# Spreading the score levels of a pair of heads over the next pair's projections in a one-core HGRN2 block

## The chip, the cores and the metric

The kernel runs on one core of one Trainium2 chip, in fp32. The metric is device time in microseconds (us) of one execution. TensorE (PE) does the matmuls, VectorE (DVE), ScalarE (ACT) and GpSimd (POOL) the elementwise work, and SyncE (SP) issues the DMAs of the part looked at here. Each engine runs its own list of instructions strictly in order and waits on semaphores for what the others have to deliver.

## The reference

One block of a diffusion transformer, batch 1, 512 tokens, width 2048. Cut to what matters here:

```
px = modulate(x, sh1, sc1) @ w_in          # q, v, f forward, f backward, g, pool, conv
k   = (1 - lb) * sigmoid(-z);  f = lb + (1 - lb) * sigmoid(z)     # forget gates, both directions
# HGRN2, 8 heads of 128, both directions, on silu(q):
S_t = f_t * S_(t-1) + k_t v_t^T ;  o_t = q_t S_t ;  o = o_f + flip(o_b)
o   = rmsnorm(o) * norm_w * silu(g)
loc = [pool_mixer(px_pool), px_bg * dwconv3(px_cg * px_h)]      # rows of 64 tokens
yx  = [o, loc] @ w_out                     # 1024 + 512 + 512 columns
x   = layer_norm(ALPHA * x + g1 * yx);  conv FFN;  layer_norm
mod = silu(c) @ w_ada + b_ada              # sh1, sc1, g1, sh2, sc2, g2
```

## The kernel before

The program is one long run of stages, and the change lies in one of them, from about 380 to 1054 us of the span: the heads and the local mixers. In it PE computes the projections of `x`, 256 columns at a time. One projection (`proj_x`) has four quarters; a quarter loads 512 rows of weights (`wload`: a DMA to `wr`, a rounded copy `wh` on ACT, the rest `wl` on DVE), calls `background()`, and then issues its matmuls. Each product of fp32 numbers is three matmuls (`mm3`, lines 111 to 113), so a quarter has 24 matmuls of 512 columns, or 48 of 256 columns for `v`, whose result has the tokens on the partitions.

The heads are taken in four pairs. A pair has the projections q, v, g, f forward and f backward (the first pair's v and f were computed in an earlier stage, so it has q and g alone). After them comes the attention of the pair (`gla`, a generator for each head). It builds the 128x128 score blocks from seven **levels** m = 1, 2, 4, ... 64. At a level:

- ACT copies the keys of the level into `kc` (L569), PE makes the scores `lv` from `kc` and `Q` (L573, four matmuls of 128x128), and DVE writes them under a mask into `A` (`copy_predicated`, L648; at m = 1 ACT writes `A` and DVE adds the diagonal `dg`);
- DVE multiplies `Q` by the decays `T` (L589), POOL does the same to the two halves of `K` (L592, L593), and DVE multiplies pairs of decays into the next, half as long `T` (L594). The next level of the head needs `Q` and `K` of this one.

Behind the levels there is a **tail** of five steps: the keys are transposed (`kTp`, L605), the state increments `U` and the states `S` made (L611, L617), the output `o` (L625 to 627), its norm `on` on ACT and DVE (L636), the transpose `oT` (L641) and `ot` (L643).

In `heads` both heads' seven levels are issued in one go, when the pair's projections have been issued. The tails are run by `background()`, one step at each quarter of the next projections, the second head three quarters behind the first (TAIL_LAG). The scheduler may move instructions within what the data allow, and puts some matmuls of the next projection between the levels.

`background()` also draws three steps at each quarter from `ada_rest`, which computes the later columns of `mod`: a step is a 256 KB load `a` on SP's queue into one of six buffers and one DVE instruction `aacc` (L688, the first of a group of sixteen L686); each group ends in small matmuls `a2r`, `a2c`.

Behind the last pair come `local` (two pool projections with their window sums, then two groups of conv projections cg, ch, cb) and `split_o`, which splits the 16 tiles of the output for the last projection.

Of the kernel before, what the change touches and what calls it, by code (L numbers as in the profile page):

```python
# [36 lines left out]
TAIL_LAG = 3  # L37
# [35 lines left out]
class Kernel:  # L73
# [436 lines left out]
    def heads(self, xp, gp, T0, V0):  # L510
        nc = self.nc
        for p in range(4):
            qs, Qs, gs = [], [], []
            b = self.proj_x(f"q{p}", 256 * p)
            for h in range(2):
                sg = gp.tile([P, L], F32, name=f"sq_{p}_{h}", tag="sig", bufs=1)
                nc.scalar.activation(out=sg, in_=b[h], func=AF.Sigmoid)
                q = gp.tile([P, L], F32, name=f"q_{p}_{h}", tag="q", bufs=2)
                nc.vector.tensor_tensor(out=q, in0=b[h], in1=sg, op=ALU.mult)
                qs.append(q)  # L520
            if p == 0:
# [12 lines left out]
            if p > 0:
                T = [xp.tile([P, 2, L], F32, name=f"T_{2 * p + h}", tag="t", bufs=2) for h in range(2)]
            K = [xp.tile([P, 2, L], F32, name=f"K_{2 * p + h}", tag="k", bufs=2) for h in range(2)]
            for d in range(2):
                zs = [t[:, 1 - d] for t in T]
                if p > 0:
                    zs = self.proj_x(f"f{d}{p}", DH * (2 + d) + 256 * p)  # L540
                for h in range(2):
                    self.gates(zs[h], T[h], K[h], d, d * H + 2 * p + h)
            for h in range(2):
                Q = gp.tile([P, 2, L], F32, name=f"Q_{p}_{h}", tag="Q", bufs=2)
                nc.vector.tensor_tensor(out=Q, in0=vw(qs[h][:, :], [[0, 2], [1, L]]), in1=T[h], op=ALU.mult)
# [12 lines left out]
    def gla(self, gp, hd, q, Q, K, T, V, gs):
# [179 lines left out]

    def local(self, gp):
        nc, I = self.nc, self.I  # L740
        pw = gp.tile([P, 4, P], F32, name="pool_w", tag="q", bufs=2)
        nc.sync.dma_start(out=pw, in_=I["pool_w"][0].rearrange("g p q -> p g q"))
        inv = gp.tile([P, 4, 64], F32, name="inv", tag="inv", bufs=1)
        nc.sync.dma_start(out=inv, in_=I["k_inv"])
        R = L // 64
        for p in range(2):
            b = self.proj_x(f"pool{p}", 5 * DH + 256 * p)
            for i in range(2):
                g = 2 * p + i
                win = POOL_WINDOWS[g]  # L750
                W = 64 + win
                pad = gp.tile([P, R, W], F32, name=f"pad_{g}", tag="Q", bufs=2)
                nc.gpsimd.memset(pad, 0.0)
                nc.vector.tensor_copy(out=pad[:, :, win // 2:win // 2 + 64],
                                      in_=b[i].rearrange("p (r t) -> p r t", t=64))
                src, s = pad, 1

                tmp = gp.tile([P, R, W], F32, name=f"win_{g}", tag="Q", bufs=2)
                sums = tmp
                wlen = W  # L760
                while s < win:
                    wlen -= s
                    nc.vector.tensor_tensor(out=sums[:, :, 0:wlen], in0=src[:, :, 0:wlen], in1=src[:, :, s:s + wlen],
                                            op=ALU.add)
                    src = sums
                    s *= 2
                dd = gp.tile([P, R, 64], F32, name=f"pd_{g}", tag="gs", bufs=2)
                nc.vector.tensor_tensor(out=dd, in0=sums[:, :, 0:64], in1=vw(inv[:, g], [[0, R], [1, 64]]), op=ALU.mult)
                nc.vector.tensor_tensor(out=dd, in0=dd, in1=pad[:, :, win // 2:win // 2 + 64], op=ALU.subtract)
                py = self.glbank(f"py_{g}")  # L770
                nc.tensor.matmul(out=py, lhsT=pw[:, g], rhs=dd.rearrange("p r t -> p (r t)"), start=True, stop=True)
                o = gp.tile([P, L], F32, name=f"op_{g}", tag="o", bufs=16)
                nc.scalar.activation(out=o, in_=py, func=AF.Copy, scale=self.cols["pool_scale"][:, g:g + 1])
                self.o[H + g] = o
        cw = self.cols["conv_w"]
        base = 5 * DH + 512
        for p in range(2):
            b = self.proj_x(f"cg{p}", base + 512 + 256 * p)
            cg = []
            for i in range(2):  # L780
                t = gp.tile([P, L], F32, name=f"cg_{p}_{i}", tag="A", bufs=2)
                nc.scalar.copy(out=t, in_=b[i])
                cg.append(t)
            b = self.proj_x(f"ch{p}", base + 1024 + 256 * p)
            ys = []
            for i in range(2):
                n = 2 * p + i
                nc.vector.tensor_tensor(out=cg[i], in0=b[i], in1=cg[i], op=ALU.mult)
                y = gp.tile([P, L], F32, name=f"cy_{p}_{i}", tag="o", bufs=16)
                nc.scalar.activation(out=y, in_=cg[i], func=AF.Copy, scale=cw[:, 4 + n:5 + n])  # L790
                c3 = cg[i].rearrange("p (r t) -> p r t", t=64)
                y3 = y.rearrange("p (r t) -> p r t", t=64)
                nc.vector.scalar_tensor_tensor(out=y3[:, :, 1:64], in0=c3[:, :, 0:63], scalar=cw[:, n:n + 1],
                                               in1=y3[:, :, 1:64], op0=ALU.mult, op1=ALU.add)
                nc.vector.scalar_tensor_tensor(out=y3[:, :, 0:63], in0=c3[:, :, 1:64], scalar=cw[:, 8 + n:9 + n],
                                               in1=y3[:, :, 0:63], op0=ALU.mult, op1=ALU.add)
                ys.append(y)
            b = self.proj_x(f"cb{p}", base + 256 * p)
            for i in range(2):
                nc.vector.tensor_tensor(out=ys[i], in0=b[i], in1=ys[i], op=ALU.mult)  # L800
                self.o[H + 4 + 2 * p + i] = ys[i]
# [373 lines left out]
    def run(self):  # L1175
# [76 lines left out]
```

## Time and profile before

| what | value |
| --- | --- |
| median of three executions | 2699.03 us (2696.9 to 2702.64) |
| profiled execution: its time, its span | 2703.39 us, 2701.6 us |
| PE busy in the span | 2573.6 us (95%) |
| DVE / ACT / POOL busy | 1895.1 (70%) / 941.6 (35%) / 225.7 us (8%) |
| PE's granted clock, mean | 0.989 |
| chain that ended last, largest shares | PE 69%, DVE 14%, DMA 8%, issue 5% |

Times in rows are counted from the span's start. A row of the timeline gives start and length of an instruction (or of a run of like ones), its engine and source line, and in brackets how long the engine stood idle ahead of it and what ended that. The end of a matmul is modelled: one follows another closer than its length. The granted clock is given as a share of full speed.

### The profile page before, as it was taken

The page shows a single profiled execution, that of the slowest core. Times are in us where ns is not written, and L with a number is a line of the kernel's source. Part 1 is how long each engine was busy: PE and PEld are TensorE (multiplying, and loading weights), DVE is VectorE, ACT ScalarE, POOL GpSimd, SP SyncE. Part 2 cuts the span into 40 slices and gives each one's busy share as a digit, 9 for nine tenths or more (in the row PEclk, how much of TensorE's full clock was granted, in tenths as well). Part 3 has the DMA queues.
Part 4 walks back from the last instruction along what each step waited for, and adds up shares of the span by engine and source line. Part 5 has one row for each costly group of instructions (what it writes and reads, how often), then busy time and mean ns, then how long its engine had stood idle before and what let it go on. Part 6 is the DMA issues. An engine that isn't in the chain of part 4 may idle for free.

```text
span 2701.6 us, 40017 instructions
## 1 busy us (share of the span) xinstructions
PE 2573.6 (95%) x16332; PEld 2261.4 (84%) x16332; DVE 1895.1 (70%) x2390; ACT 941.6 (35%) x1127; POOL 225.7 (8%) x207
## 2 busy tenths in 40 slices
PE   5999999999999999989979999999999999999996
PEld 4677978878787787868879999999999988888885
DVE  5534689696968735688888888888888864434338
ACT  4222443232323224444644443443443433222111
POOL 0111022040404000000100000000000000000004
PEclk9999999999999999999989999999999999999998
DMA  8755356646463534666633333333333374333321
GB/s 265 250 194 187 121 198 199 218 136 214 138 221 131 169 97 160 204 213 212 189 104 125 126 103 124 122 106 119 109 122 114 117 245 161 136 121 119 118 94 63
DMA packets 311125, 416.15 MB, mean 154 GB/s; under 512 B 17860, under 2 KB 200476, under 8 KB 310428
## 3 DMA queue, kind: packets, MB, share of 16 engines
q1 hardware_dynamic: 310940, 413.59, 46.6%
q8 instruction: 128, 2.10, 0.3%
q14 instruction: 57, 0.47, 0.0%
HBM read 393.59 MB, written 19.93 MB: 153 GB/s over the span
## 4 chain that ended last, share of the span: by engine, by line
PE 69%; DVE 14%; DMA 8%; issue 5%; ACT 2%; POOL 1%; SPq 1%; DVEq 0%; ACTq 0%; POOLq 0%
PE dn L113 5%; PE dn L112 5%; PE dn L111 5%; PE ub_g L111 3%; PE ub_g L113 3%; PE ub_g L112 3%; DMA W_u<-in_w_up_dram 3%; PE ub_u L111 3%; PE ub_u L113 3%; PE ub_u L112 3%; DMA W_g<-in_w_up_dram 2%; DVE L_g L973 2%; PE wo L112 2%; PE wo L111 2%; PE wo L113 2%
## 5 line engine op out<-in xcount | busy, mean ns | idle before, releaser
L973 DVE TENSOR_TENSOR L_dn<-W_dn,H_dn 128x1536 fp32r<-128x1536 f32 (+1 forms) x56 | 96.2, 1718 | 207.9 <-ACT H_dn L972 207.9
L972 ACT CAST H_u<-W_u 128x1792 fp32r<-128x1792 f32 x80 | 134.1, 1692 | 230.2 <-DVE W_u L991 158.2
L688 DVE SCALAR_TENSOR_TENSOR aacc<-a,csil,aacc 128x512 f32<-128x512 f32 x240 | 180.2, 751 | 12.9 <-DMA a<-in_w_ada_dram 7.5
L973 DVE TENSOR_TENSOR L_u<-W_u,H_u 128x1792 fp32r<-128x1792 f32 x80 | 161.6, 2020 | 38.0 <-ACT H_u L972 38.0
L111 PE MATMUL dn<-H_dn,hh 128*128 128x512 f32 x480 | 186.4, 389 | 1.4 <-ACT hh L1070 1.4
L112 PE MATMUL dn<-L_dn,hh 128*128 128x512 f32 x480 | 187.0, 390 | 0.0
L113 PE MATMUL dn<-H_dn,hl 128*128 128x512 f32 x480 | 186.7, 390 | 0.0
L972 ACT CAST H_g<-W_g 128x1792 fp32r<-128x1792 f32 x80 | 135.2, 1695 | 123.4 <-DVE W_g L991 46.0
L972 ACT CAST H_dn<-W_dn 128x1536 fp32r<-128x1536 f32 (+1 forms) x56 | 81.3, 1451 | 276.2 <-PE dn L113 275.3
L973 DVE TENSOR_TENSOR L_g<-W_g,H_g 128x1792 fp32r<-128x1792 f32 x80 | 161.4, 2018 | 2.4 <-ACT H_g L972 2.4
L111 PE MATMUL ub_g<-h2h,H_g 128*128 128x256 f32 x480 | 135.6, 283 | 14.9 <-ACT H_g L972 14.9
L125 POOL TENSOR_TENSOR ln_r<-ln_e,mhalf 128x1 f32<-128x1 f32 x12 | 9.3, 784 | 1636.0 <-DVE ln_e L120 1405.6
L113 PE MATMUL ub_g<-h2h,L_g 128*128 128x256 f32 x480 | 135.5, 283 | 4.5 <-DVE L_g L973 4.5
L113 PE MATMUL ub_u<-h2h,L_u 128*128 128x256 f32 x480 | 134.3, 280 | 4.4 <-DVE L_u L973 4.4
L112 PE MATMUL ub_g<-h2l,H_g 128*128 128x256 f32 x480 | 134.9, 281 | 0.0
L111 PE MATMUL ub_u<-h2h,H_u 128*128 128x256 f32 x480 | 134.6, 280 | 0.0
L112 PE MATMUL ub_u<-h2l,H_u 128*128 128x256 f32 x480 | 133.9, 279 | 0.0
L106 DVE TENSOR_TENSOR wl_wo<-wr_wo,wh_wo 128x1024 fp32r<-128x1024 f32 x64 | 78.3, 1223 | 49.4 <-ACT wh_wo L105 49.3
L111 PEld LDWEIGHTS dn<-H_dn,hh 128*128 128x128 f32 x480 | 90.1, 188 | 20.6 <-ACT hh L1070 1.8
L113 PEld LDWEIGHTS dn<-H_dn,hl 128*128 128x128 f32 x480 | 90.1, 188 | 19.3 <-DVE hl L1071 0.6
L112 PE MATMUL wo<-wl_wo,oh 128*128 128x512 f32 x256 | 102.7, 401 | 3.7 <-DVE wl_wo L106 3.6
L112 PEld LDWEIGHTS dn<-L_dn,hh 128*128 128x128 f32 x480 | 90.1, 188 | 19.2 <-DVE L_dn L973 0.4
(445 smaller groups left out, 8370.7 us busy)
## 6 DMA issues: line engine op xcount, KB each, us to landing
a<-in_w_ada_dram SPq DMA_DIRECT2D x256, 256.0 KB, 4.3
W_g<-in_w_up_dram SPq DMA_DIRECT2D x80, 512.0 KB, 4.6
W_u<-in_w_up_dram SPq DMA_DIRECT2D x80, 512.0 KB, 4.6
W_dn<-in_w_down_dram SPq DMA_DIRECT2D x24, 1536.0 KB, 6.8
wr_wo<-in_w_out_dram SPq DMA_DIRECT2D x64, 512.0 KB, 4.4
ada<-in_w_ada_dram SPq DMA_DIRECT2D x56, 512.0 KB, 5.0
wr_r<-in_w_in_dram SPq DMA_DIRECT2D x48, 512.0 KB, 3.7
wr_up<-in_w_up_dram SPq DMA_DIRECT2D x32, 512.0 KB, 4.5
```

Source lines behind the costliest of these rows:

```text
L106: (lo_engine or nc.vector).tensor_tensor(out=lo, in0=raw, in1=hi.bitcast(F32), op=ALU.subtract)
L111: mm(out=out, lhsT=st[0], rhs=mv[0], start=start, stop=False)
L112: mm(out=out, lhsT=st[0], rhs=mv[1], start=False, stop=False)
L113: mm(out=out, lhsT=st[1], rhs=mv[0], start=False, stop=stop)
L125: nc.gpsimd.tensor_tensor(out=r, in0=t, in1=self.mhalf[:, 0:n], op=ALU.pow)
L688: nc.vector.scalar_tensor_tensor(out=acc, in0=raw, scalar=self.csil[:, k:k + 1], in1=acc, op0=ALU.mult, op1=ALU.add)
L972: nc.scalar.copy(out=H[:, 0:n], in_=src)
L973: nc.vector.tensor_tensor(out=Lw[:, 0:n], in0=src, in1=H[:, 0:n].bitcast(F32), op=ALU.subtract)
```

## The change

The two generators of a pair are no longer driven through their levels in `heads`. They are kept in `self.steps`, and `background()` advances them: in each of the next seven quarters both heads make one level, after that the tails follow as before, one step a quarter, the second head three quarters behind. So the levels of pair 0, 1 and 2 lie beside q and v of the following pair, and those of the last pair beside the first conv projections. `local` is cut in two functions and its order becomes conv 0, pool 0, pool 1, conv 1.

The rest makes room for what now lives longer: `q` and `g` tiles come from the 16 buffers of the outputs (tag "o"), `pool_w` and `pd` have buffers of their own, and the conv's `cg` lies in tiles of a pool that the split of the outputs uses too. What is computed is the same.

```diff
@@ heads
-                q = gp.tile([P, L], F32, name=f"q_{p}_{h}", tag="q", bufs=2)
+                q = gp.tile([P, L], F32, name=f"q_{p}_{h}", tag="o", bufs=16)
...
-                g = gp.tile([P, L], F32, name=f"g_{p}_{h}", tag="gs", bufs=2)
+                g = gp.tile([P, L], F32, name=f"g_{p}_{h}", tag="o", bufs=16)
...
-            steps = [self.gla(gp, 2 * p + h, qs[h], Qs[h], K[h], T[h], V[:, :, h * P:(h + 1) * P], gs[h])
-                     for h in range(2)]
-            for _ in range(len(LEVELS)):
-                for st in steps:
-                    next(st)
-            self.tails, self.bg_calls = steps, 0
-        for st in self.tails:
-            for _ in st:
-                pass
+            self.steps = [self.gla(gp, 2 * p + h, qs[h], Qs[h], K[h], T[h], V[:, :, h * P:(h + 1) * P], gs[h])
+                          for h in range(2)]
+            self.bg_calls = 0
@@ background
-        if self.tails:
-            next(self.tails[0], None)
-            if self.bg_calls >= TAIL_LAG:
-                next(self.tails[1], None)
-            self.bg_calls += 1
+        n, self.bg_calls = self.bg_calls, self.bg_calls + 1
+        if self.steps:
+            next(self.steps[0], None)
+            if n < len(LEVELS) or n >= len(LEVELS) + TAIL_LAG:
+                next(self.steps[1], None)
         self.bg_due += 3.0
@@ local
-        pw = gp.tile([P, 4, P], F32, name="pool_w", tag="q", bufs=2)
+        pw = gp.tile([P, 4, P], F32, name="pool_w", tag="pw", bufs=1)
...
+        self.conv(gp, 0)
+        self.pool(gp, 0, pw, inv)
+        self.pool(gp, 1, pw, inv)
+        self.conv(gp, 1)
...
-                dd = gp.tile([P, R, 64], F32, name=f"pd_{g}", tag="gs", bufs=2)
+            dd = gp.tile([P, R, 64], F32, name=f"pd_{g}", tag="pd", bufs=2)
...
-                t = gp.tile([P, L], F32, name=f"cg_{p}_{i}", tag="A", bufs=2)
+            t = self.a2(f"cg_{p}_{i}", F32)
@@ run
                     self.local(gp)
-                    for _ in self.bg:
-                        pass
+                    for st in (self.bg, *self.steps):
+                        for _ in st:
+                            pass
                     self.split_o()
```

What this does to PE's list behind pair 0 is shown by the rows around level 2 of heads 0 and 1 (`lv_0_2`, `lv_1_2`); `px_q1_0` and `px_q1_1` are the two banks of the next pair's q projection, and a name ends in a running number. Before:

```order
L573 MATMUL lv_0_2_3698<-Q_0_0_3648,kc_0_2_3696 128x128 x4
L573 MATMUL lv_1_2_3710<-Q_0_1_3650,kc_1_2_3708 128x128 x4
L113 MATMUL px_q1_1_3841<-hxh_0_354,wl_x_q1_0_3845 128x512
L111 MATMUL px_q1_0_3840<-hxh_1_639,wh_x_q1_0_3844 128x512
L112 MATMUL px_q1_0_3840<-hxl_1_640,wh_x_q1_0_3844 128x512
L113 MATMUL px_q1_0_3840<-hxh_1_639,wl_x_q1_0_3845 128x512
L573 MATMUL lv_0_4_3722<-Q_0_0_3648,kc_0_4_3720 128x128 x4
L111 MATMUL px_q1_1_3841<-hxh_1_639,wh_x_q1_0_3844 128x512
L573 MATMUL lv_1_4_3734<-Q_0_1_3650,kc_1_4_3732 128x128 x4
```

and after the change:

```order
L111 MATMUL px_q1_1_3653<-hxh_3_756,wh_x_q1_0_3656 128x512
L112 MATMUL px_q1_1_3653<-hxl_3_757,wh_x_q1_0_3656 128x512
L113 MATMUL px_q1_1_3653<-hxh_3_756,wl_x_q1_0_3657 128x512
L567 MATMUL lv_0_2_3748<-Q_0_0_3648,kc_0_2_3746 128x128 x4
L567 MATMUL lv_1_2_3760<-Q_0_1_3650,kc_1_2_3758 128x128 x4
L111 MATMUL px_q1_0_3652<-hxh_4_1003,wh_x_q1_1_3742 128x512
L112 MATMUL px_q1_0_3652<-hxl_4_1004,wh_x_q1_1_3742 128x512
```

Level 2 now stands behind the whole first quarter (24 matmuls, three of them shown; before it stood behind three), and 24 matmuls of the next quarter lie between it and level 4, where four lay.

On DVE the same place reads, before:

```order
L648 COPY_PREDICATED A_0_3652<-masks_652,lv_0_2_3698 128x512
L589 TENSOR_TENSOR Q_0_0_3648<-Q_0_0_3648,T2_0_3653 128x128x2x2
L648 COPY_PREDICATED A_1_3674<-masks_652,lv_1_2_3710 128x512
L589 TENSOR_TENSOR Q_0_1_3650<-Q_0_1_3650,T2_1_3675 128x128x2x2
L594 TENSOR_TENSOR T_1_270<-T2_1_3675 128x2x128
L648 COPY_PREDICATED A_0_3652<-masks_652,lv_0_4_3722 128x512
L589 TENSOR_TENSOR Q_0_0_3648<-Q_0_0_3648,T_0_269 128x64x2x4
```

and after the change (a2_2_3 is load `a` number 3 of group 2, `wl_x_q1_3` the weights of a later quarter):

```order
L106 TENSOR_TENSOR wl_x_q1_2_3806<-wr_x_q1_2_3803,wh_x_q1_2_3805 128x1024
L642 COPY_PREDICATED A_0_3660<-masks_652,lv_0_2_3748 128x512
L583 TENSOR_TENSOR Q_0_0_3648<-Q_0_0_3648,T2_0_3661 128x128x2x2
L642 COPY_PREDICATED A_1_3682<-masks_652,lv_1_2_3760 128x512
L583 TENSOR_TENSOR Q_0_1_3650<-Q_0_1_3650,T2_1_3683 128x128x2x2
L588 TENSOR_TENSOR T2_0_3661<-T_0_269 128x2x64
L588 TENSOR_TENSOR T2_1_3683<-T_1_270 128x2x64
L683 SCALAR_TENSOR_TENSOR aacc_1_3504<-a2_1_15_3836,csil_154,aacc_1_3504 128x512
L683 SCALAR_TENSOR_TENSOR aacc_2_3839<-a2_2_2_3900,csil_154,aacc_2_3839 128x512
L683 SCALAR_TENSOR_TENSOR aacc_2_3839<-a2_2_3_3903,csil_154,aacc_2_3839 128x512
L683 SCALAR_TENSOR_TENSOR aacc_2_3839<-a2_2_4_3971,csil_154,aacc_2_3839 128x512
L106 TENSOR_TENSOR wl_x_q1_3_3870<-wr_x_q1_3_3867,wh_x_q1_3_3869 128x1024
```

Where the copies and products of one level followed those of the level before at once, there now stand a weight split `wl` and four `aacc` between two levels.

## Rows read from the trace of the kernel before

**Rows 1.** Busy time by stretch. The columns are the stretch, its length, busy us and instructions of PE, of PE's weight load, of DVE, ACT and POOL, PE's granted clock, the share of the DMA engines' time and GB/s. The stretches are the levels of pair 0, the projections of pair 1, and the levels of pairs 1 and 3.

```profile
380.00:430.00 50.00, 44.71 (x259) 37.29 (x258) 46.82 (x72) 15.58 (x25) 25.61 (x27) 0.97 0.45 149
430.00:540.00 110.00, 110.00 (x634) 95.32 (x633) 77.16 (x115) 31.30 (x56) 3.04 (x3) 1.00 0.74 243
540.00:580.00 40.00, 33.88 (x212) 26.97 (x211) 39.88 (x59) 14.76 (x24) 31.74 (x30) 1.00 0.15 45
...
838.00:880.00 42.00, 35.92 (x227) 29.15 (x225) 38.60 (x56) 13.83 (x22) 31.04 (x30) 1.00 0.15 47
```

**Rows 2.** What PE waited for from 380 to 1060 us: idle us in all, number of waits, the longest.

```profile
PE lv L573 <- DVE Q L589: 12.9, 25, 3.6
PE lv L573 <- DVE Q L545: 4.6, 6, 1.1
PE lv L573 <- ACT kc L569: 4.5, 8, 1.6
PE lv L573 <- DVE T L594: 1.9, 3, 0.6
PE oT L641 <- DVE on L636: 1.8, 2, 0.9
```

**Rows 3.** PE's timeline in the levels of pair 1, about level 16.

```profile
563.13 0.40 PE L113 MATMUL px_q<-hxh,wl_x_q 128*128 128x512 f32 x1
563.69 1.13 PE L573 MATMUL lv<-Q,kc 128*128 128x128 f32 x8 [0.16 <-DVE Q L589]
564.57 0.47 PE L111 MATMUL px_q<-hxh,wh_x_q 128*128 128x512 f32 x1
```

**Rows 4.** PE's timeline and the stretches (columns as in rows 1) in pair 0, at level 2.

```profile
399.90 3.52 PE L573 MATMUL lv<-Q,kc 128*128 128x128 f32 x16 [3.59 <-DVE Q L589]
403.08 0.77 PE L113 MATMUL px_q<-hxh,wl_x_q 128*128 128x512 f32 x1
...
404.05 0.39 PE L112 MATMUL px_q<-hxl,wh_x_q 128*128 128x512 f32 x1
...
396.00:400.00 4.00, 0.41 (x3) 0.13 (x2) 4.00 (x5) 0.86 (x2) 4.00 (x4) 1.00 0.41 122
400.00:404.00 4.00, 4.00 (x18) 3.63 (x19) 4.00 (x6) 1.08 (x2) 3.47 (x4) 0.58 0.31 112
```

**Rows 5.** PE's timeline where the levels of pair 1 begin, and one row of pair 3.

```profile
543.76 1.56 PE L573 MATMUL lv<-Q,kc 128*128 128x128 f32 x8 [1.10 <-DVE Q L545]
...
547.12 1.56 PE L573 MATMUL lv<-Q,kc 128*128 128x128 f32 x8 [0.45 <-DVE Q L545]
...
552.16 1.08 PE L573 MATMUL lv<-Q,kc 128*128 128x128 f32 x7 [0.97 <-DVE Q L589]
...
849.96 1.23 PE L573 MATMUL lv<-Q,kc 128*128 128x128 f32 x8 [1.55 <-ACT kc L569]
```

**Rows 6.** DVE's timeline in one level of pair 1, both heads.

```profile
562.12 0.73 DVE L648 COPY_PREDICATED A<-masks,lv 128x512 f32<-128x512 uint8 x1
562.75 0.79 DVE L589 TENSOR_TENSOR Q<-Q,T 128x512 f32<-128x512 f32 x1
563.47 0.66 DVE L594 TENSOR_TENSOR T<-T 128x64 f32<-128x64 f32 x1
564.05 0.73 DVE L648 COPY_PREDICATED A<-masks,lv 128x512 f32<-128x512 uint8 x1
...
565.94 0.73 DVE L648 COPY_PREDICATED A<-masks,lv 128x512 f32<-128x512 uint8 x1
```

**Rows 7.** DVE's and POOL's timelines at the last levels of pair 1.

```profile
576.84 0.67 DVE L589 TENSOR_TENSOR Q<-Q,T 128x512 f32<-128x512 f32 x1
577.43 0.16 DVE L594 TENSOR_TENSOR T<-T 128x8 f32<-128x8 f32 x1
...
569.86 0.62 POOL L592 TENSOR_TENSOR K<-K,T 128x256 f32<-128x256 f32 x1 [0.19 <-DVE T L594]
570.44 1.07 POOL L593 TENSOR_TENSOR K<-K,T 128x256 f32<-128x256 f32 x1
```

**Rows 8.** PE's timeline in a quarter of an f projection and at the end of one of v.

```profile
500.17 0.39 PE L111 MATMUL px_f<-hxh,wh_x_f 128*128 128x512 f32 x1
...
505.61 0.39 PE L111 MATMUL px_f<-hxh,wh_x_f 128*128 128x512 f32 x1
...
597.15 0.28 PE L112 MATMUL px_v<-wl_x_v,hxh 128*128 128x256 f32 x1
597.27 0.28 PE L113 MATMUL px_v<-wh_x_v,hxl 128*128 128x256 f32 x1
```

**Rows 9.** A weight split on DVE's timeline in an f projection, and L688 by its source line (least, median and greatest length in ns).

```profile
505.31 1.23 DVE L106 TENSOR_TENSOR wl_x_f<-wr_x_f,wh_x_f 128x1024 fp32r<-128x1024 f32 x1 [4.22 <-ACT wh_x_f L105]
...
L688 DVE SCALAR_TENSOR_TENSOR aacc<-a,csil,aacc x228: 736/752/1046, 380.1 to 947.8; 128x512 f32<-128x512 f32 x114
```

**Rows 10.** DVE's timeline at the beginning of pair 0's levels.

```profile
394.62 1.05 DVE L688 SCALAR_TENSOR_TENSOR aacc<-a,csil,aacc 128x512 f32<-128x512 f32 x1 [1.70 <-DMA a<-in_w_ada_dram]
395.59 1.88 DVE L106 TENSOR_TENSOR wl_x_q<-wr_x_q,wh_x_q 128x1024 fp32r<-128x1024 f32 x1
397.39 0.68 DVE L532 TENSOR_TENSOR g<-px_g,g 128x512 f32<-128x512 f32 x1
...
398.60 2.63 DVE L589 TENSOR_TENSOR Q<-Q,T 128x512 f32<-128x512 f32 x2
```

More of the change, by code (lines that the diff above doesn't have):

```diff
@@ L744, in local @@
         nc.sync.dma_start(out=inv, in_=I["k_inv"])
-        R = L // 64
[L746 to L766, printed above, removed]
-                dd = gp.tile([P, R, 64], F32, name=f"pd_{g}", tag="gs", bufs=2)
[L768 to L774, printed above, removed]
@@ new lines, in local, with pool @@
+        self.conv(gp, 0)
+        self.pool(gp, 0, pw, inv)
+        self.pool(gp, 1, pw, inv)
+        self.conv(gp, 1)
+    def pool(self, gp, p, pw, inv):
+        nc = self.nc
+        R = L // 64
+        b = self.proj_x(f"pool{p}", 5 * DH + 256 * p)
+        for i in range(2):
+            g = 2 * p + i
+            win = POOL_WINDOWS[g]
+            W = 64 + win
+            pad = gp.tile([P, R, W], F32, name=f"pad_{g}", tag="Q", bufs=2)
+            nc.gpsimd.memset(pad, 0.0)
+            nc.vector.tensor_copy(out=pad[:, :, win // 2:win // 2 + 64],
+                                  in_=b[i].rearrange("p (r t) -> p r t", t=64))
+            src, s = pad, 1
+            tmp = gp.tile([P, R, W], F32, name=f"win_{g}", tag="Q", bufs=2)
+            sums = tmp
+            wlen = W
+            while s < win:
+                wlen -= s
+                nc.vector.tensor_tensor(out=sums[:, :, 0:wlen], in0=src[:, :, 0:wlen], in1=src[:, :, s:s + wlen],
+                                        op=ALU.add)
+                src = sums
+                s *= 2
+            dd = gp.tile([P, R, 64], F32, name=f"pd_{g}", tag="pd", bufs=2)
+            nc.vector.tensor_tensor(out=dd, in0=sums[:, :, 0:64], in1=vw(inv[:, g], [[0, R], [1, 64]]), op=ALU.mult)
+            nc.vector.tensor_tensor(out=dd, in0=dd, in1=pad[:, :, win // 2:win // 2 + 64], op=ALU.subtract)
+            py = self.glbank(f"py_{g}")
+            nc.tensor.matmul(out=py, lhsT=pw[:, g], rhs=dd.rearrange("p r t -> p (r t)"), start=True, stop=True)
+            o = gp.tile([P, L], F32, name=f"op_{g}", tag="o", bufs=16)
+            nc.scalar.activation(out=o, in_=py, func=AF.Copy, scale=self.cols["pool_scale"][:, g:g + 1])
+            self.o[H + g] = o
@@ L775, in local, with conv @@
+    def conv(self, gp, p):
+        nc = self.nc
         cw = self.cols["conv_w"]
         base = 5 * DH + 512
[L777 to L780, printed above, removed]
-                t = gp.tile([P, L], F32, name=f"cg_{p}_{i}", tag="A", bufs=2)
[L782 to L801, printed above, removed]
@@ new lines, in conv @@
+        b = self.proj_x(f"cg{p}", base + 512 + 256 * p)
+        cg = []
+        for i in range(2):
+            t = self.a2(f"cg_{p}_{i}", F32)
+            nc.scalar.copy(out=t, in_=b[i])
+            cg.append(t)
+        b = self.proj_x(f"ch{p}", base + 1024 + 256 * p)
+        ys = []
+        for i in range(2):
+            n = 2 * p + i
+            nc.vector.tensor_tensor(out=cg[i], in0=b[i], in1=cg[i], op=ALU.mult)
+            y = gp.tile([P, L], F32, name=f"cy_{p}_{i}", tag="o", bufs=16)
+            nc.scalar.activation(out=y, in_=cg[i], func=AF.Copy, scale=cw[:, 4 + n:5 + n])
+            c3 = cg[i].rearrange("p (r t) -> p r t", t=64)
+            y3 = y.rearrange("p (r t) -> p r t", t=64)
+            nc.vector.scalar_tensor_tensor(out=y3[:, :, 1:64], in0=c3[:, :, 0:63], scalar=cw[:, n:n + 1],
+                                           in1=y3[:, :, 1:64], op0=ALU.mult, op1=ALU.add)
+            nc.vector.scalar_tensor_tensor(out=y3[:, :, 0:63], in0=c3[:, :, 1:64], scalar=cw[:, 8 + n:9 + n],
+                                           in1=y3[:, :, 0:63], op0=ALU.mult, op1=ALU.add)
+            ys.append(y)
@@ L803, in split_o @@
+        b = self.proj_x(f"cb{p}", base + 256 * p)
+        for i in range(2):
+            nc.vector.tensor_tensor(out=ys[i], in0=b[i], in1=ys[i], op=ALU.mult)
+            self.o[H + 4 + 2 * p + i] = ys[i]
     def split_o(self):
@@ L1193, in run @@
                 with tc.tile_pool(name="gp", bufs=1) as gp:
-                    self.bg, self.bg_due, self.tails = self.ada_rest(gp), 0.0, []
+                    self.bg, self.bg_due, self.steps, self.bg_calls = self.ada_rest(gp), 0.0, [], 0
                     self.heads(xp, gp, T0, V0)
                     self.local(gp)
-                    for _ in self.bg:
-                        pass
+                    for st in (self.bg, *self.steps):
+                        for _ in st:
+                            pass
                     self.split_o()
```

## The prediction

> **What bounds the kernel now.** I read the stretches first [rows 1]. In a pair's projections PE is busy for all of 110 us while DVE works 77. In a pair's levels DVE is busy for 39.88 of 40 us and PE idles 6.12 (pair 1); 5.29 in pair 0, 6.08 in pair 3. So the stage alternates between a PE-bound and a DVE-bound regime, and what the levels cost is PE's idle time. The waits say who ends it [rows 2]: nearly all lies ahead of `lv`, 12.9 us in 25 waits for the product Q of L589, 4.6 in 6 for the first Q, 4.5 in 8 for `kc`, 1.9 in 3 for T. Two waits of `oT` hold 1.8 us.
>
> An idle bracket understates the loss, since a matmul's end is modelled. At 563.13 a projection matmul starts; the next thing starts at 563.69 with 0.16 in its bracket [rows 3]. Undisturbed matmuls start 0.227 apart (24 from 500.17 to 505.61, [rows 8]), so the loss is 0.56 - 0.227 = 0.33, or 0.17 more than shown. The 42 waits of `lv` therefore lose 23.9 + 42 x 0.165 = 30.8 us, `oT` 1.8 + 2 x 0.165 = 2.1. Together 32.9.
>
> One more loss: behind the 3.59 us wait of pair 0 the granted clock is 0.58 from 400 to 404 [rows 4], a mean near the lower of its levels (1.2 of 2.4 GHz). Sixteen `lv` passes took 403.08 - 399.90 = 3.18 us; eight take 564.57 - 563.69 = 0.88 at full clock [rows 3], so about 1.8 with a little for the start, 1.9. Two projection matmuls took 404.05 - 403.08 = 0.97 for 0.45. That makes 1.3 + 0.5, about 1.7 with rounding. **Loss before: 34.6 us.**
>
> **The change, part by part.** PE's instructions are the same in number, so the question is how much of 34.6 us is left.
>
> *Time per level.* PE has one quarter and one level of two heads from level to level: 24 x 0.227 = 5.44 (q, conv) plus two times 0.88, so 7.2 us; for v 48 x 0.12 (597.15 to 597.27, [rows 8]) plus 1.76, 7.55. DVE's level of both heads takes 565.94 - 562.12 = 3.8 us [rows 6]. To it come a weight split of 1.22 [rows 9] and some `aacc`, 0.775 each in a row (0.752 the median length, [rows 9], and a little for the issue). The order has four or five `aacc` between most levels, so DVE needs 3.8 + 1.22 + 4 x 0.775 = 8.1 or, with five, 8.9. That is more than PE's 7.2. DVE thus stays the slower engine while levels run, but by about 1 us a level instead of by all its work: the levels no longer come as a lump.
>
> *Pair 0.* Before, DVE is at its first Q products from 398.60 for 2.63 us, to 401.2 [rows 10]. In the new order a mask copy (0.63), six `aacc`, a first `aacc` (0.4) and two T products (0.4 each) stand ahead of the split for quarter 2: 401.2 + 6.5 = 407.7, less the 0.8 of one `aacc` that stood earlier before; about 407. The Q that level 4 needs follows at 407 + 1.22 + 0.63 + 0.75 = 409.6. PE gets there earlier: 21 matmuls (4.8 us) fill what is now the wait before 399.90, level 2 goes at 401.2, and 24 matmuls later, at 408, level 4 waits 2 us, counting the second head. Then come four gaps: DVE 8.1, 8.9, 9.5 (with two products for silu like the 0.68 at 397.39, and four `aacc`) and 8.6 (one of the `aacc` a short first one), 35.1 in all; PE 7.15 + 7.15 + 7.55 + 7.55 = 29.4. Stall: 2 + 5.7 = **7.7**. With the 3.59 us wait gone the clock does not fall: 1.7 becomes 0.
>
> *Pairs 1 and 2.* The first waits stay, as PE's order there is the old one (first level of one head, two projection matmuls, first level of the other): 1.10 + 0.45 + 0.97 + 3 x 0.165 = 3.0 [rows 5]. Later a Q may come 5.44 + 0.88 = 6.3 us after its level's scores; copies and products of both heads and the split take 2.7 + 1.2 = 3.9, so 2.4 are in hand. The gaps that count have five `aacc` (one short), four, and four with two q products: 8.6, 8.1 and 9.5 against 7.15 each, 4.75 over, less 2.4 in hand: 2.4 lost. **5.4 each.**
>
> *Pair 3,* beside conv 0: 1.10 + 0.46 + 1.55 (`kc`, [rows 5]) + 0.5 = 3.6; then gaps with no `aacc` twice, six and four: 9.7 and 8.1 against 7.15, 3.5 over less 2.4: 1.1. **4.7.**
>
> *The tails.* `oT` now has 24 projection matmuls behind `o`, 5.4 us of cover for the norm: 2.1 becomes 0.
>
> *The rest at nothing.* The window sums, the conv and the tails' states keep their work and only change place, under projections where DVE waits up to 4.22 us for each split [rows 9]; uncovered, a split's 1.22 would be late by as much. `pool_w`'s load is issued early on SP's queue, 256 KB like one `a`, with the DMA share at 0.15 in the levels [rows 1]. The split of the first output tiles, which moves to the end because `cg` takes its tiles, is DVE and ACT work beside full projections as well. The loads `a` come evenly now instead of stopping in a lump, and were late before by 1.70 at most [rows 10].
>
> **Sum.** After: 7.7 + 5.4 + 5.4 + 4.7 = 23.2. Before 34.6. Gain 11.4, so the profiled 2703.39 becomes 2692.0, and the median, 4.4 lower than that execution, 2699.0 - 11.4 = 2687.6; I say **2687**.
>
> **What is not known: POOL against DVE.** The 3.8 us of a level were measured with POOL busy 31.74 of 40 us [rows 1]. T products take 0.58 from start to start beside POOL's work [rows 6] and 0.16 when it is idle, Q 0.67 for 0.79; a POOL product lasts 0.62 alone and 1.07 beside DVE [rows 7]. So either may hold the other. Spread out, POOL works four products of 0.62, 2.5 us, in each level of 7 to 9. If it never meets DVE, a level costs DVE 2 x (0.63 + 0.62 + 0.16) = 2.8: 1 us less in each of some 13 gaps that count, and only the first waits and 3 us of pair 0 remain, 12.7 in all; gain 22, 2677. If each product of POOL holds up an `aacc` or a split in full, the level costs 2.8 + 4 x 0.62 = 5.3, 1.45 more than I took in 13 gaps: 19 more, 42 in all, 2707. I keep 3.8, the row itself, because the four products meet some instruction of DVE whichever it is.
>
> The Trainium skill ("SBUF — State Buffer", section "Who interferes with whom") speaks against the change here: a DVE instruction with two inputs in SBUF contends with a GpSimd instruction that reads SBUF, and the one that issues first has the ports for its whole length. `aacc` and the weight split have two such inputs. The 1.88 us of a split beside POOL at 395.59 against 1.22 agrees [rows 9, 10]. By the page every `aacc` could be held once, and the sum would be the one with 5.3, by the row 3.8.
>
> **Rivals.**
> *Slower: POOL's products hold DVE in full.* Place: the `aacc` and splits between levels. Price: up to 1.45 a gap. It decides from 11.4 / 13 = 0.9 us a gap on; at the full price 42 - 34.6 = 7.5 slower, 2707. For it: the split of 1.88 and an `aacc` of 1.05 [rows 10]. Against it: 0.752 is the median of the `aacc`, and the lump's 3.8 already holds the worst of it. By the page's lock this is what a spread POOL does, each product meeting a two-input instruction. Chance 0.13.
> *No change: DVE is saturated.* DVE does the same work either way. If a late `a` (1.7, [rows 10]) or a late split (PE then lacks weights) costs 0.5 to 1 us a level more than the sum has, 13 gaps take back 6 to 12 us: 2693 to 2700. For it: DVE's 8.1 to 9.5 exceed PE's 7.2 everywhere. Against it: beyond the levels DVE has 33 us to spare in each pair's projections, and nothing queued there is urgent. Chance 0.20.
> *Better: POOL out of the way.* 2.8 to 3.3 a level: 2675 to 2681. For it: the uncontended rows [rows 7]. Chance 0.17.
> *The forecast,* 2681 to 2693, has 0.50.
>
> **How the numbers follow.** About 0.2%, 5.4 us, is what a measurement here can tell from no change. Faster is forecast and better, 0.67; same 0.20; slower 0.13. The range reaches from the better case's 2677 to 2701, beyond no change, and leaves out part of the better case (0.07) and most of slower (0.11). Within faster alone it is 2677 to 2693.
>
> **What would show it.** In the profile after: no 3.59 us wait in pair 0 and a granted clock of 1.00 there; `oT` out of the list of waits; waits of `lv` for Q still in the list with 12 to 17 us, most in pair 0; first waits of 1.1, 0.45 and 1.0 unchanged; T products nearer 0.16 where POOL is done, and `aacc` longer than 0.752 where it is not. DVE between two levels at 8 to 9 us would confirm the sum; below 7 the better case; a median `aacc` near 1 us or splits of 1.9 the slower one. A new wait of projection matmuls for `wl` would make the forecast wrong.

## The result and the profile after

The changed kernel takes 2682.81 us in the median of four executions (2678.45 to 2688.15), beside 2699.47 for the kernel before on the same chip. The ratio is 0.9935 with a 95% interval of 0.9917 to 0.9953: 17 us faster, where 12 were forecast, and inside the range. The profiled execution has a span of 2686.4 us.

The stage that was changed can be measured more sharply than the whole program, from PE's first matmul of the second pair's q to its first of the output projection. Before, these start at 392.59 and 1054.73. PE's timeline after:

```profile
392.97 0.48 PE L111 MATMUL px_q<-hxh,wh_x_q 128*128 128x512 f32 x1
...
1036.02 0.39 PE L111 MATMUL wo<-wh_wo,oh 128*128 128x512 f32 x1
```

So the stage went from 662.1 to 643.0 us: 19.1 gained. Everything behind it took 1646.9 us before and 1650.4 after, with the same instructions. How far such a number wanders is seen below, where one kernel was profiled twice (e6 and e9): stage 641.5 and 640.5, span 2679.9 and 2690.0. From here on the stage is compared, and the time where it was taken in several executions.

PE's waits from 380 to 1060 us in the changed kernel (idle us, number, longest), to be held against [rows 2]:

```profile
PE lv L567 <- DVE Q L545: 4.6, 6, 1.1
PE lv L567 <- DVE Q L583: 4.4, 7, 1.0
PE a2c L701 <- DVE A L642: 2.2, 1, 2.2
PE lv L567 <- ACT wh_x_v L105: 1.0, 1, 1.0
```

The waits for the product Q of a level (L589 before, L583 now) fell from 12.9 us in 25 to 4.4 in 7. Those for `kc` and T are gone, `oT` too. The first waits of each pair (L545) are untouched. The 1.0 put down to `wh_x_v` stands ahead of level 16 of pair 0, at 428.18; the Q product of that level had ended only at 428.04, so it is a wait for DVE as well. One row is new: `a2c`.

Busy time by stretch, for [rows 1] (same columns; pairs 0, 1 and 3):

```profile
380.00:430.00 50.00, 46.76 (x245) 39.27 (x245) 46.69 (x63) 15.78 (x23) 21.39 (x19) 0.97 0.74 237
540.00:580.00 40.00, 36.53 (x226) 31.42 (x225) 39.68 (x51) 13.49 (x20) 26.78 (x25) 1.00 0.44 130
...
838.00:880.00 42.00, 41.02 (x234) 35.30 (x233) 38.41 (x56) 13.16 (x19) 24.09 (x25) 1.00 0.47 146
```

DVE is as busy as it was, but PE's idle time in these stretches is 3.2, 3.5 and 1.0 us instead of 5.3, 6.1 and 6.1. What moved in is seen in the DMA share, 0.44 for 0.15: the loads `a` now run beside the levels.

### The profile page after: what moved, and what is told of

Its sections match the earlier page's. It is cut to its first block, busy times and chain, and to the rows that moved or that the text cites. A ratio compares the mean times of both kernels' runs of the same rounds, so it can differ in the third digit from the quotient of the medians.

```text
span 2686.4 us, 40001 instructions
## 1 busy us (share of the span) xinstructions
PE 2568.8 (96%) x16332; PEld 2264.9 (84%) x16332; DVE 1893.9 (70%) x2390; ACT 939.8 (35%) x1127; POOL 234.9 (9%) x207
## 4 chain that ended last, share of the span: by engine, by line
PE 62%; DVE 17%; DMA 11%; issue 5%; ACT 2%; POOL 1%; SPq 1%; DVEq 0%; POOLq 0%; ACTq 0%
PE dn L112 5%; PE dn L111 5%; PE dn L113 5%; DMA W_u<-in_w_up_dram 4%; DMA W_g<-in_w_up_dram 3%; PE ub_g L113 2%; DVE L_g L976 2%; PE ub_g L111 2%; PE ub_g L112 2%; DVE L_u L976 2%; PE ub_u L111 2%; PE ub_u L113 2%; PE ub_u L112 2%; PE px_f L111 2%; PE wo L112 2%
## 5 line engine op out<-in xcount | busy, mean ns | idle before, releaser
L683 DVE SCALAR_TENSOR_TENSOR aacc<-a,csil,aacc 128x512 f32<-128x512 f32 x240 | 188.1, 784 | 10.6 <-DMA a<-in_w_ada_dram 5.2
L113 PEld LDWEIGHTS dn<-H_dn,hl 128*128 128x128 f32 x480 | 90.1, 188 | 19.7 <-DVE hl L1074 0.9
```

Of the source, the lines that this page charges most:

```text
L113: mm(out=out, lhsT=st[1], rhs=mv[0], start=False, stop=stop)
L683: nc.vector.scalar_tensor_tensor(out=acc, in0=raw, scalar=self.csil[:, k:k + 1], in1=acc, op0=ALU.mult, op1=ALU.add)
```

## Where VectorE's time between two levels goes

DVE's timeline in pair 0, one gap between two levels of the changed kernel:

```profile
407.68 1.70 DVE L106 TENSOR_TENSOR wl_x_q<-wr_x_q,wh_x_q 128x1024 fp32r<-128x1024 f32 x1
409.30 0.73 DVE L642 COPY_PREDICATED A<-masks,lv 128x512 f32<-128x512 uint8 x1
409.93 1.16 DVE L583 TENSOR_TENSOR Q<-Q,T 128x512 f32<-128x512 f32 x1
411.01 0.73 DVE L642 COPY_PREDICATED A<-masks,lv 128x512 f32<-128x512 uint8 x1
411.64 0.68 DVE L583 TENSOR_TENSOR Q<-Q,T 128x512 f32<-128x512 f32 x1
412.23 0.48 DVE L588 TENSOR_TENSOR T<-T 128x128 f32<-128x128 f32 x2
412.64 3.25 DVE L683 SCALAR_TENSOR_TENSOR aacc<-a,csil,aacc 128x512 f32<-128x512 f32 x4
415.81 1.66 DVE L106 TENSOR_TENSOR wl_x_q<-wr_x_q,wh_x_q 128x1024 fp32r<-128x1024 f32 x1
417.39 0.73 DVE L642 COPY_PREDICATED A<-masks,lv 128x512 f32<-128x512 uint8 x1
```

From copy to copy it is 8.09 us; the sum had 8.1. But its parts are not those of the sum: the level itself takes 3.3 us (409.30 to 412.64), not 3.8, and the split 1.66, not 1.22. GpSimd's products now meet the split and the first Q product (1.16 for 0.68). The second question is what this meeting costs in all, in the spread and in the lump. That is what the runs without GpSimd's products ask.

## The experiments

**e1: the lump, with the rest of the change.**

```diff
+            for _ in range(len(LEVELS)):
+                for st in self.steps:
+                    next(st)
-            self.bg_calls = 0
+            self.bg_calls = len(LEVELS)
```

> The changed kernel with one part undone: the seven levels of a pair are issued in a lump again as before, while the order of the mixers, the buffers of q, g, pool_w, pd and cg, and the tails' place stay as changed. Stage length is counted from PE's first matmul of the second pair's q to its first of the output projection (662.1 us before, 643.0 after). Theory 1, the spreading makes the gain: 658 to 664 here, and a time within 0.2% of before; at most the 2 us of the two oT waits differ. Theory 2, the new order of the mixers and the buffers make a good part of it: below 655.

Measured: stage 658.9 us, ratio to before 0.9991 (0.9981 to 1.0001). The new order of the mixers and the buffers brings about 3 us of the stage. Theory 1 stands: the spreading makes the other 16 of the 19.1.

**e2 and e3: no products on GpSimd, in the spread and in the lump.** Both lines are left out, so K keeps its undecayed values and the scores come from those.

```diff
-            nc.gpsimd.tensor_tensor(out=kf, in0=kf, in1=vw(cur, [[2, nb], [0, m]], ts_ + 1), op=ALU.mult)
-            nc.gpsimd.tensor_tensor(out=kb, in0=kb, in1=vw(cur, [[2, nb], [0, m]]), op=ALU.mult)
```

> The changed kernel without the two products on GpSimd that carry K from level to level (left out: the decay of K, so the scores are those of undecayed keys). GpSimd then has next to nothing to do beside the levels. Theory 1, GpSimd's products lengthen VectorE's instructions wherever they meet, in the spread too: the weight splits beside levels fall from 1.6 to 1.22, the first Q product of a level from 1.1 to 0.67, VectorE's step in pair 0 from 8.1 and 9.4 to below 7.6 and 8.5, the waits of lv for Q of L583 from 4.4 to below 2 us, the stage from 643.0 to 637 to 640. Rival, GpSimd alone is held up and VectorE is not: same lengths, steps and stage within 1 us.

> The kernel before without the same two products on GpSimd (left out: the decay of K). Theory 1, contention is part of the lump's price: a level on VectorE falls from 3.8 to 2.8 to 3.0 us, the waits of lv for Q of L589 from 12.9 to below 8 us, those for kc vanish, the stage from 662.1 to 645 to 652. Rival, GpSimd alone is held up: levels stay at 3.8 and the stage gets shorter by the 4.5 us of kc at most, 657 to 662.

Measured, in one execution each: stage 628.8 us in the spread and 633.9 in the lump. Both moved further than expected, the lump by 28.2, the spread by 14.3. DVE's timeline of one level of both heads in e3, pair 1, to be held against [rows 6]:

```profile
551.54 0.74 DVE L646 COPY_PREDICATED A<-masks,lv 128x512 f32<-128x512 uint8 x1
552.17 0.67 DVE L589 TENSOR_TENSOR Q<-Q,T 128x512 f32<-128x512 f32 x1
552.76 0.21 DVE L592 TENSOR_TENSOR T<-T 128x64 f32<-128x64 f32 x1
552.90 0.73 DVE L646 COPY_PREDICATED A<-masks,lv 128x512 f32<-128x512 uint8 x1
553.53 0.67 DVE L589 TENSOR_TENSOR Q<-Q,T 128x512 f32<-128x512 f32 x1
554.12 0.22 DVE L592 TENSOR_TENSOR T<-T 128x64 f32<-128x64 f32 x1
554.47 0.74 DVE L646 COPY_PREDICATED A<-masks,lv 128x512 f32<-128x512 uint8 x1
```

A level takes 2.9 us instead of 3.8. PE's list has the same projection matmuls between the levels in both kernels (32 behind the second level of pairs 1 to 3, 29 in pair 0), so only the lengths differ, and PE's waits show what that does:

```profile
PE lv L573 <- DVE Q L545: 3.4, 3, 1.1
PE lv L573 <- DVE Q L589: 2.4, 1, 2.4
PE oT L639 <- DVE on L634: 1.7, 2, 0.9
```

One wait for Q of L589 is left out of 25, none for `kc`. The 32 stand in five gaps of four to nine: in the mean, 6.4 matmuls of 0.227 and two groups of scores of 0.88 make 3.2 us of PE work between two levels, enough for a level of 2.9 and not for one of 3.8. In the spread the same gap as above reads

```profile
404.76 1.22 DVE L106 TENSOR_TENSOR wl_x_q<-wr_x_q,wh_x_q 128x1024 fp32r<-128x1024 f32 x1
405.90 0.72 DVE L640 COPY_PREDICATED A<-masks,lv 128x512 f32<-128x512 uint8 x1
406.52 0.68 DVE L583 TENSOR_TENSOR Q<-Q,T 128x512 f32<-128x512 f32 x1
...
408.73 2.99 DVE L681 SCALAR_TENSOR_TENSOR aacc<-a,csil,aacc 128x512 f32<-128x512 f32 x4
411.63 1.22 DVE L106 TENSOR_TENSOR wl_x_q<-wr_x_q,wh_x_q 128x1024 fp32r<-128x1024 f32 x1
412.77 0.73 DVE L640 COPY_PREDICATED A<-masks,lv 128x512 f32<-128x512 uint8 x1
```

6.87 us from copy to copy instead of 8.09. So the lump without GpSimd's products is 9 us shorter than the spread with them, and spreading is worth 5.1 us without them (633.9 to 628.8) and 19.1 with them.

Leaving the products out removes two things at once: the lengthening of DVE's instructions and the chain through GpSimd to `kc`. DVE's own busy time tells them apart. From the first Q product of pair 1 to its last mask copy, in the kernel before and in e3 (columns as in [rows 1]):

```profile
542.40:576.22 33.82, 27.70 (x177) 21.68 (x175) 33.82 (x46) 11.57 (x18) 30.38 (x29) 1.00 0.12 37
536.65:562.42 25.77, 24.54 (x168) 22.20 (x167) 25.39 (x45) 11.20 (x17) 1.33 (x1) 1.00 0.13 37
```

In the kernel before DVE is busy for the whole stretch: it waits for nobody, not for `kc` and not for PE. The same instructions take it 8.1 us less in e3, and 8.2 and 7.8 less in pairs 2 and 3, 24.1 in all. In pair 0 it takes 16.5 us from the first mask copy of `lv` to the last instead of 21.3. Together that is 28.9 us, enough for the whole 28.2 of the stage: the price was the lengthened instructions, and the waits for `kc` only show where PE stood while DVE was behind.

**e4: no `aacc` beside the levels.**

```diff
-        self.bg_due += 3.0
+        self.bg_due += 0.0 if self.steps and n < len(LEVELS) else 4.0
```

> The changed kernel with no step of the background sums drawn in the seven quarters that carry levels, and four instead of three in the others (their number in all is the same). Theory 1, the gaps are VectorE's sum of level, split and aacc: its step falls from 8.1 to about 5, all waits of lv for Q of L583 but the first two of each pair's start vanish, about 3 us, and the stage goes to 638 to 641 if the other quarters have room for a fourth aacc. Rival, gaps are set by the chain of scores, copy and Q product itself: waits for L583 stay at 4 us or more.

Measured: stage 642.6 us, no gain. Waits for L583 are 3.5 us in four, but those for the first Q grew from 4.6 to 6.0 and a first `kc` came with 1.6. At the start of pair 2, where one wait is 2.4, an `aacc` of 0.74 us stands between the gates (681.87), and the first Q product takes 1.85 us for 1.22. Thinning the background alone only moves the wait.

**e5: one quarter later.**

```diff
-        if self.steps:
+        if self.steps and n >= 1:
             next(self.steps[0], None)
-            if n < len(LEVELS) or n >= len(LEVELS) + TAIL_LAG:
+            if n < len(LEVELS) + 1 or n >= len(LEVELS) + TAIL_LAG + 1:
```

> The changed kernel with the levels starting one quarter later: nothing of the pair in the first quarter, level 1 in the second, and all that follows one quarter later. Stage length as before (662.1 before, 643.0 changed). If what the changed kernel still loses at each pair's start (1.10 + 0.45 + 0.97 us shown, 3.0 with what the brackets leave out, three times) is only the chain from the last gate to the first Q products, one quarter of 5.44 us covers it, and pair 0's wait of 2.19 us with its low clock goes too: 643.0 less 9 to 13, so 630 to 634, and 2669 to 2675 us. Rival: the wait moves to the second and later levels, as VectorE is as late one quarter on: 640 to 644.

Measured: stage 641.9 us. Level 1 of pair 0 now lies behind the first q matmul; counted from the first pair's first g matmul, which is 24.5 us earlier in the other kernels, the fairer number is 639.9 (664.4 - 24.5). 2680.97 us, ratio 0.9928 (0.9911 to 0.9944), the same as the changed kernel's. The rival holds. PE's waits:

```profile
PE lv L567 <- DVE Q L583: 4.4, 5, 1.2
PE lv L567 <- DVE Q L545: 3.7, 5, 2.0
```

Pair 0's `a2c` is gone, but the first Q still waits and a quarter's head start does not help where DVE's gap is longer than PE's.

**e6, e7, e9 and e10: K on VectorE.** One instruction of 128x512 for each head and level does both products, nothing is left out. e6 and e9 have it in the kernel before, e7 and e10 in the changed one.

```diff
-            nc.gpsimd.tensor_tensor(out=kf, ...)
-            nc.gpsimd.tensor_tensor(out=kb, ...)
+            kv = vw(Ka, [[2 * m, nb], [L + m, 2], [1, m]])
+            nc.vector.tensor_tensor(out=kv, in0=kv, in1=vw(cur, [[2, nb], [-ts_ - 1, 2], [0, m]], ts_ + 1), op=ALU.mult)
```

> The kernel before with the two products of K done by one VectorE instruction per head and level instead of two on GpSimd, nothing left out. Theory after the runs without these products (stage 634.0 in a lump, 628.7 spread): the lump's loss came from GpSimd and VectorE in each other's way. Without GpSimd a level costs VectorE 2.9, with the K product 2 x 0.67 more, 4.2; PE then waits 4.2 - 2.9 longer in about 24 levels, 634 + 31 = 665: no better than before, 655 to 668. Rival: the chain through GpSimd and kc was the lump's price, not VectorE's time: 640 to 650.

> The changed kernel with the two products of K as one VectorE instruction per head and level. The step without them was 6.9 to 7.8 us in pair 0; with 1.34 more it is 8.2 to 9.1, as with GpSimd. Stage 638 to 644, no clear change from 643.0. Rival: GpSimd costs more than its own 1.34 a step since it also delays the first Q products of each pair: 632 to 637.

> The kernel before with K on VectorE again, now timed. One look gave a stage of 641.4 us, within 2 us of the changed kernel's 643.0, with the levels still in a lump: 2680 to 2685 us and a ratio of 0.992 to 0.996 if that holds. If the look was an outlier, the ratio is above 0.997.

> The changed kernel with K on VectorE again, now timed beside e9. Stage 634.0 in one look, 7 us below the lump with K on VectorE: 2672 to 2678 us. If spreading adds nothing once GpSimd is out of the way, the two times agree within 3 us.

Measured: the lump has a stage of 641.5 and 640.5 us and, timed, 2688.16 us (ratio 0.9950, 0.9931 to 0.9970), slower than the 2680 to 2685 expected of e9; the spread 634.0 and 633.9 and 2678.48 (0.9913, 0.9886 to 0.9939), where 2672 to 2678 was expected of e10. The two intervals overlap slightly, so that the spread is faster here rests on the stages. For both I had first expected no gain, and both were missed: e6 and e7 landed in the ranges of their rivals. In e7 DVE's step in pair 0 is 7.16 us (copies at 402.58 and 409.74) and not 8.2, with three `aacc` in the gap and a split of 1.22, and PE's first waits fall to 3.4 us in three. In e6 the reason that the rival gave, the chain through `kc`, is not the cause, since DVE did not wait in the kernel before. Nor is DVE faster: pair 1 takes it 36.41 us from the first Q product (538.64) to the last mask copy (575.05), 33.82 before, and a level 3.9 to 5.6. What differs is PE's list. Behind the second head's level 2 it now has 61 projection matmuls between the levels of pairs 1 to 3 where it had 32, and so PE's waits in e6 are short:

```profile
PE oT L639 <- DVE on L634: 4.3, 5, 0.9
PE lv L573 <- DVE Q L545: 3.4, 3, 1.1
PE lv L573 <- DVE Q L589: 2.7, 1, 2.7
PE lv L573 <- ACT kc L569: 0.2, 1, 0.2
```

The lump is not bad in itself. It loses where the order puts less PE work between two levels than the level takes on the chip. With K on GpSimd the level is longer than the 3.2 us put there; with K on DVE there are 61 / 5 x 0.227 + 1.76 = 4.5, close to the 4.75 that a level takes DVE in the mean (551.28 to 575.05, five levels). Spreading gives 6.5 to 7.5 us on top of that. A lump with this list and K on GpSimd was not run, so how much of e6's gain needs K on DVE stays open.

**e11: two levels a quarter.**

```diff
-            next(self.steps[0], None)
-            if n < len(LEVELS) or n >= len(LEVELS) + TAIL_LAG:
-                next(self.steps[1], None)
+            for _ in range(2 if n < 3 else 1):
+                next(self.steps[0], None)
+                if n < 4 or n >= 4 + TAIL_LAG:
+                    next(self.steps[1], None)
```

> The changed kernel with two levels of both heads a quarter for the first three quarters, then one; GpSimd keeps its products. Theory, what counts is the PE work between two levels against VectorE's level with GpSimd beside it: 12 matmuls and a level's scores are 2.7 + 1.76 = 4.5 us, VectorE's level with half a split and half the aacc is 3.8 + 0.6 + 1.2 = 5.6, so about 1.1 lost in some five gaps a pair less 2.4 in hand, 3 a pair, and the tails follow earlier: stage 648 to 656, between the changed kernel's 643.0 and the lump's 658.9 with the same order of mixers. Rival, any spreading over quarters gives the whole gain: 641 to 645.

Measured: stage 660.5 us, no gain over e1's 658.9, so this was missed too.

```profile
PE lv L567 <- DVE Q L583: 16.3, 13, 3.0
PE lv L567 <- DVE Q L545: 4.6, 6, 1.1
PE lv L567 <- ACT kc L563: 2.6, 5, 0.9
```

The split and the `aacc` of a quarter don't share themselves out over its two levels: they all fall into one gap. DVE's steps from copy to copy in pair 1 are 3.1, 4.9, 7.8, 3.2 and 8.9 us. PE's list has 4, 6, 13, 8 and 16 projection matmuls in these gaps, with the scores 2.7, 3.1, 4.7, 3.6 and 5.4 us: the two long gaps lose over 3 us each. My expectation had put the mean on each.

**e8: later, thinner, and K on VectorE.** The three edits of e5, e7 and a milder form of e4 (1.5 steps beside levels, 3.6 else).

> All that the runs point to together: levels one quarter later, K on VectorE, and 1.5 instead of 3 background steps in the quarters with levels (3.6 in the others). VectorE's step is 2.8 + 1.34 + 1.22 + 1.5 x 0.775 = 6.5 us against 7.2 of PE, so no wait between levels is left: stage 622 to 628, 2663 to 2670 us. Rival: the thicker background in the f quarters delays the weight splits and the gates at each pair's end, as without aacc beside the levels: 630 to 638.

Measured: 2672.25 us, ratio 0.9898 (0.9884 to 0.9913), stage 628.0, and 654.4 - 24.5 = 629.9 by the fairer count of e5: 13.2 below the changed kernel and 32.3 below before. The time is 2 us above the range expected. PE's waits, and a stretch behind the second of them (columns as in [rows 1]):

```profile
PE lv L567 <- DVE Q L545: 2.1, 3, 1.1
PE a2r L690 <- DVE aacc L681: 2.1, 1, 2.1
PE wo L112 <- DVE wl_wo L106: 0.6, 1, 0.6
...
384.00:388.00 4.00, 4.00 (x18) 3.06 (x11) 3.86 (x6) 0.27 (x1) 0.00 (x0) 0.57 0.99 348
```

No wait between two levels is left. The wait for `aacc` is new and stands at 383.78, ahead of the second pair's q, so only the fairer count has it. With the low clock behind it, PE's way from the first g to the first q matmul takes 26.3 us where e5 has 22.5: 3.9 us that I put down to the thicker background beside the other projections. This is the fastest version here; its interval and that of the changed kernel do not overlap.

| stage, us | lump | spread | spread, later and thinner |
| --- | --- | --- | --- |
| K on GpSimd | 662.1 (e1: 658.9) | 643.0 | |
| K on VectorE | 641.5, 640.5 | 634.0, 633.9 | 629.9 |
| K left out | 633.9 | 628.8 | |

## Why the prediction was right, and where its sum was not

The direction and the mechanism were right: PE waits for DVE in the lump, and spreading takes most of that away. The size was not. The stage gained 19.1 us for 11.4 forecast. That the time came within 4.2 us of 2687 was luck in part, since 3.5 us were lost again behind the stage, where nothing was changed.

*The loss before, 34.6 us,* was too small. From the first pair's first g matmul on, PE has the same number of instructions in all these kernels, and e8 takes 32.3 us less than before. e8 itself still loses 2.6 us in three waits for Q (2.1 shown) and 3.9 at its `a2r`. So an estimate of the loss before is 32.3 + 2.6 + 3.9 = 38.8, 4.2 more than the waits and the clock held.

*The loss after, 23.2 us,* was too large. The kernel after takes 13.2 us more than e8, so by the same estimate it loses 13.2 + 6.5 = 19.7. By the waits of the stage's levels it is less: 12.4 us shown in 16, with 0.165 for each that the bracket leaves out 15.0, and 1.8 for a low clock, 16.8. The gain by these terms is 34.6 - 16.8 = 17.8. So the step that was mis-sized is the loss after, with DVE's level put at 3.8 us in every gap: 23.2 for 16.8 by the waits. Its parts:

- *Pair 0, 7.7:* 5.3 by the rows, and of another kind. I had let 21 projection matmuls fill the old wait. They stand behind `a2c` in PE's list, and `a2c` waits for DVE's mask copy. PE's timeline there:

```profile
398.43 0.39 PE L701 MATMUL a2c<-sel,a2s 128*128 128x4 f32 x2 [2.19 <-DVE A L642]
398.68 0.56 PE L111 MATMUL px_q<-hxh,wh_x_q 128*128 128x512 f32 x1
399.03 0.63 PE L112 MATMUL px_q<-hxl,wh_x_q 128*128 128x512 f32 x1
399.46 0.63 PE L113 MATMUL px_q<-hxh,wl_x_q 128*128 128x512 f32 x1
```

  and the stretch from 398.4 to 402.4 (columns as in [rows 1]):

```profile
398.40:402.40 4.00, 3.97 (x11) 3.16 (x12) 4.00 (x5) 0.14 (x1) 3.82 (x4) 0.57 0.57 193
```

  The granted clock is 0.57 behind the wait, near the lower of its two levels (1.2 of 2.4 GHz), and matmuls start 0.43 us apart instead of 0.227: nine of them cost 1.8 us. So "the clock does not fall" was wrong, and the row for `a2c` stood in the new order to be read. PE came to level 2 at 405.15, not 401.2, and this hid the waits that I had put at levels 4 and 8.
- *The gaps.* DVE's steps in pair 0 are 8.09, 9.35, 8.00 and 7.94 us for 8.1, 8.9, 9.5 and 8.6. The first agrees, the second is 0.5 longer. In the later ones a level takes 2.5 (from the copy at 426.75 to the first `aacc` at 429.27), as GpSimd has finished before; the 3.8 of [rows 6] was too much there.
- *Pairs 1 and 2, 5.4 each:* 4.8 and 3.7 by the same count. The first waits stayed as said (2.3 and 2.5 us shown), and the gaps cost 1.8 and 0.7, with what the brackets leave out, where 2.4 was expected.
- *Pair 3, 4.7:* 3.0. The wait for `kc` at its start did not come back and no gap waits.
- *`oT`, 2.1 to 0:* right.

*The unknown, GpSimd against VectorE.* I kept 3.8 for a level with the reason that the products meet some instruction of DVE whichever it is. That holds for the step: 8.09 with them, 6.87 without, 1.2 us a gap. It was the right size for the first two gaps and too much for the rest. (The 0.16 of a T product that the better case used was of 128x8; those of 128x64 take 0.21 in e3.) The Trainium skill ("SBUF — State Buffer", section "Who interferes with whom") says that VectorE's instructions with two inputs in SBUF contend with GpSimd's reads. The rows agree: splits and Q products are longer beside GpSimd (1.66 for 1.22, 1.16 for 0.68), the mask copy with its scores from PSUM has a median of 0.73 us in the changed kernel and in the kernel before. The rival with every `aacc` held once did not come, because few meet a product: between 390 and 900 us of the changed kernel 42 of 210 do, by their times in the trace, and those take 1.00 us in the median where the others take 0.75.

*What I had wrong about the cause.* I read the lump as a regime that DVE's work bounds. e3 shows the same lump, with PE's list alike between the levels, without these waits: DVE's own work, 2.9 us a level, fits into the 3.2 that PE has between two levels. The lump was bound by DVE with GpSimd in its way, and by an order that puts too little PE work between two such levels. Of the 19.1 us gained, 14.0 need GpSimd's products to be there. The forecast was right since it took the price of a level from the row and not from its cause.

*What was to be seen.* Right: no wait of 3.59, `oT` gone, first waits unchanged, T products at a median of 0.216 us (0.614 before), DVE's step at 8 to 9 us. Not right: the clock of 1.00 in pair 0, and 12 to 17 us of waits for Q; it was 9.0.

Open in part: 4.2 us of the loss before and 2.9 of the loss after that the waits and the clock don't hold. Their difference is the 1.3 us of the stage's 19.1 that is missing above. Some of it follows the waits: in pair 1 of the kernel before, the second score matmul behind a wait starts 0.18 to 0.23 us after the first, where 0.11 is usual, which over 42 waits would be some 3 us, an estimate.

## What to carry to other kernels

A lump of small dependent steps costs what each step takes beyond the work that the order puts between two of them; so count that work in the order, and take the step's length from a row in which its neighbours are busy as they will be. Before spreading such a lump, see whether an engine next to the one that binds stretches its instructions: here GpSimd's products made VectorE's level 3.8 us long for 2.9. Handing them to VectorE, which seemed to be the bound, gave nearly as much as the spreading (0.9950 beside 0.9935, with intervals that overlap), though in the lump it came with a PE list that has nearly twice the matmuls between two levels. Both together, with a start one quarter later and a thinner background, gave 1.0% of the whole. When work is spread, look for small instructions of other chains (`a2c` here) that the new order puts ahead of the work meant to fill a wait.

## What the runs showed of the hardware

- Where they meet GpSimd's products of 128x256, VectorE's instructions of two SBUF operands are longer. Medians in the changed kernel from 390 to 900 us, meeting a product and not: Q products 1.10 and 0.67 us, weight splits 1.62 and 1.22, `aacc` 1.00 and 0.75. An instruction of one SBUF operand can be held too: three `TENSOR_SCALAR` on T (L484) that meet one take 1.07 us, the other nine 0.43. GpSimd is held as well. Its first product of a level by source line (least, median and greatest ns), in the changed kernel and in the kernel before:

```profile
L586 POOL TENSOR_TENSOR K<-K,T x55: 610/1082/1949, 394.9 to 872.8; 128x256 f32<-128x256 f32 x55
```

```profile
L592 POOL TENSOR_TENSOR K<-K,T x55: 616/647/1957, 394.3 to 871.6; 128x256 f32<-128x256 f32 x55
```

  In the lump half of them ran alone; in the spread most meet something.
- One wait of 2.19 us ahead of `a2c` was followed by a granted clock of 0.57 in the next 4 us, as was one of 2.08 in e8, and about as the 3.59 us before (0.58); behind waits of 1.1 us elsewhere in the stage it stayed at 1.00.
